# VectorE's program order in the last two units of a mixture-of-experts layer, and exact BF16 parts in the tables of its route

## The chip, the cores and the metric

One core of one Trainium2 chip runs the whole program. The metric is the device time of one execution in microseconds (us), as the median of several runs. The profile is one execution taken by the hardware profiler; "the profile" and "the trace" mean that execution. Engines are called TensorE (PE; its weight loads PEld), VectorE (DVE), ScalarE (ACT), GpSimd (POOL) and SyncE (SP, which issues most DMAs).

## The reference

Two layers work on 256 latent tokens and 256 context tokens of width 1024. Layer 0 mixes tokens by a bidirectional RG-LRU and gated linear attention, layer 1 by grouped-query attention. After the mixer, each layer has a hierarchical mixture of experts (MoE). What the change touches is the MoE of layer 0, over all 512 tokens:

```
p_group = softmax(t @ wg + bg);  w_group, g = top_k(p_group, 1)
e_val, e_idx = top_k(expert logits of group g, 2)
w_exp = softmax(e_val) * w_group
out = sum over the two experts e of  w_exp[e] * ((silu(t @ w1[e]) * (t @ w3[e])) @ w2[e])
x = x + gate * out
```

There are 16 experts (4 groups of 4), width 1024, hidden width 512, FP32 weights: 100.7 MB per layer.

## The kernel before

**Units.** Layer 0's route sorts the 16 experts by their number of tokens. The eight fullest get a unit of 128 slots each; the other eight share four units, two experts with 64 slots each. The 12 units run in the order of `SEQ` (line 23), unit 11 being a shared one. A unit gathers its tokens' rows from DRAM (`fetch_x`, 1660, an indirect DMA on GpSimd's queue), transposes them (`prep_x`, 1693), multiplies by w1 and w3 (`hidden`, 1737), forms silu times product (`he`), transposes that, and multiplies by w2 (`py`). For the full experts every FP32 operand is split into a high and a low part and each product is made of three (`mm3`); the low part of the transposed hidden row is `hl`, made on VectorE. Weights come as loads of 1 MB into slots that one list serves in order (`pump`, 201); a load is issued when TensorE, or the split of it, has read the slot's old content.

**How results come back.** Units 0 to 9 scatter their weighted rows to DRAM (`yd`). The last two units keep theirs in SBUF as `yh` and `yl`, and products with a transposed one-hot matrix (`finish_moe`, 1902) bring them to the tokens. What the other units scattered is fetched per token tile (`get_parts`, 1803: eight loads of 512 KB on GpSimd's queue, once unit 9's scatter has landed) and added on VectorE (`merge`, 1813).

**The route.** `unit_cols` (566) multiplies by `w_out` one token tile at a time; between the products `tick()` runs one closure of a queue (transposes of `xres`, router logits). `add_res` (1615) adds the residual, forms the row's scale (`scale`, a power on GpSimd and three VectorE steps) and writes the normalised, modulated row `h2` (`tile_`, 935) to DRAM. For the last tile, number 3 (`LATE_T`), half of that is put off to `route_end` (980). There ranks are counted with triangular BF16 products, and `to_units` (1077) makes the tables: one-hot matrices of slots (`oh`), values (`vals`), and FP32 products of both, which give each slot its token row (`ix`) and, in `weights_of` (1120), its weight (`wgt`). `experts` sorts the experts for SP's dynamic loads; `others` makes the weights and `cnt`.

**The branch.** If some expert has more tokens than slots (`cnt` over 0), spare passes run (1776 and 1777). They don't run here, but all engines load `cnt` and branch.

**What sets the order.** A scheduler orders each engine's instructions by estimated costs, and may move them past their place in the program. Between `pin(name)` calls the engines whose letter stands in `PIN` (61; p TensorE, d VectorE, a ScalarE, g GpSimd) keep program order among the instructions issued there. Units run under `m0`, with TensorE alone kept.

Of the kernel before, what the change touches and what calls it, by code (L numbers as in the profile page):

```python
# [10 lines left out]
F32 = mybir.dt.float32  # L11
# [49 lines left out]
PIN = dict(pair='p', px='padg', re='da', tb='dag', m0='p', n1='pad', xa='pad')  # L61
# [77 lines left out]
def backbone(ctx, tc, I, out):  # L139
# [426 lines left out]
    def unit_cols(name, b, hT, done, tokens_still, tiles=range(4), halves=(0, 1), after=None, on_act=True,  # L566
# [5 lines left out]
        if by_tile:  # L572
# [177 lines left out]
    rows2 = rt.tile([P, 2, 8], F32, name="rows2")  # L750

    def load_router():
# [87 lines left out]

    def route(l, NT, tmp, stream, h2_of, router):
# [49 lines left out]
        def logits(t, hf, part=None):  # L891
# [32 lines left out]
        def both(t):  # L924
            if l == 0 and t == NT - 2 and not queue:
# [9 lines left out]
        def tile_(t, late=False):  # L935
# [19 lines left out]
            todo = []  # L955
            for n in range(2):
                a = tmp("xa2")
                dve.scalar_tensor_tensor(a, x[:, n * 512:(n + 1) * 512], rss[t], A2[i][n], op0=ALU.mult, op1=ALU.mult)

                def shift(n=n, a=a):  # L960
                    dve.tensor_tensor(hv[:, n * 64:(n + 1) * 64, :], a.rearrange("q (p k) -> q p k", k=KD),
                                      B2[i][n].rearrange("q (p k) -> q p k", k=KD), op=ALU.add)
                if late and n:
                    todo.append(shift)
                else:
                    shift()

            def rest():
                for f in todo:
                    f()  # L970
                sp.dma_start(h2d[l][t * P:(t + 1) * P, :], h2)
            if late:
                return rest
            rest()
# [5 lines left out]
    def route_end(R, l, NT, early=None):  # L980
# [15 lines left out]

        def weights():
# [13 lines left out]
            wq = [st(f"wq{k}", 1) for k in range(2)]  # L1011
# [42 lines left out]
        pos, wq = None, None  # L1054

        def others():
# [4 lines left out]
            dve.tensor_copy(pos, R.pp)  # L1061
            cnt = rt.tile([P, 1], F32, tag="cnt", name="cnt")
# [11 lines left out]
        if l:  # L1074
            others()

        def to_units():
# [13 lines left out]
            oh = split_p.tile([P, 1024], F32R, tag="hi", name="oh").bitcast(F32).rearrange("p (n s) -> p n s", n=NK)  # L1091
# [11 lines left out]
            v = rt.tile([P, NK, 3, NU], F32, tag="vals", name="vals")  # L1103
            dve.tensor_tensor(v[:, :, 2, :], iota[:, 0:NU].unsqueeze(1).to_broadcast([P, NK, NU]),
                              uk.unsqueeze(2).to_broadcast([P, NK, NU]), op=ALU.is_equal)
# [27 lines left out]
            return ix, weights_of, (slots_, [v[:, k * NT:(k + 1) * NT] for k in range(2)])  # L1133
# [1377 lines left out]
```

## Time and profile before

| what | value |
|---|---|
| three runs | 1007.88, 1012.01, 1014.98 us; median 1012.01 |
| the profiled execution | 1008.28 us |
| its span | 1006.6 us |
| TensorE busy | 905.5 us (90%) |
| VectorE busy | 540.6 us (54%) |
| ScalarE busy | 396.5 us (39%) |
| moved by DMA | 304.56 MB, 303 GB/s over the span |
| granted TensorE clock, mean | 0.960 of 2.4 GHz |

The profiled execution's time is its span and 1.7 us around it. Busy shares are averages over stages with different limits: the route is a serial stretch of small instructions, the MoE parts read 100.7 MB of weights each. What a change in one stage is worth has to be read from that stage, from what its engines wait for last. Matmuls are pipelined, so a busy TensorE is not one at its peak.

### The profile page before, as it was taken

Reading aid. Unit: us, or ns where it says so; the run is one execution under the profiler, and the core shown is the slowest. Engines: PE = TensorE matmul, PEld = TensorE weight load, DVE = VectorE, ACT = ScalarE, POOL = GpSimd, SP = SyncE. Lnnn points to the kernel's source line nnn. Section 1 sums busy time; section 2 is a strip of 40 time slices with the busy share of each in tenths; the row PEclk is TensorE's granted clock in tenths of the full one; section 3 lists DMA queues with packets and bytes.
Section 4 is the critical chain, followed back from the end, with each engine's and each line's share of the span. In section 5 each row is a group of like instructions: output and inputs, shape, how many; then the busy total and the mean of one; then the engine's idle time right before and its main releaser. Section 6 shows DMA issues by size and latency. Waiting matters only on the chain. (4 is left out here: it accounts for less than half of the span.)

```text
span 1006.6 us, 12582 instructions
## 1 busy us (share of the span) xinstructions
PE 905.5 (90%) x4565; PEld 535.6 (53%) x4565; DVE 540.6 (54%) x1040; ACT 396.5 (39%) x686; POOL 130.3 (13%) x142
## 2 busy tenths in 40 slices
PE   5999989999964989999999377999996999999997
PEld 3556456667744647457568133764574444443442
DVE  5495777458684656428468357787656111111112
ACT  3465472234322637347468104543644221121210
POOL 1011520133302112100001100133001000000000
PEclk9999999999995999999999788999998899999999
DMA  9957353488453899999998957655758699999994
GB/s 311 385 177 271 126 209 124 170 299 299 147 185 137 309 418 419 419 420 411 415 420 347 402 211 291 257 208 211 271 200 334 231 416 418 415 417 414 417 413 159
DMA packets 63166, 304.56 MB, mean 303 GB/s; under 512 B 8579, under 2 KB 17667, under 8 KB 35057
## 3 DMA queue, kind: packets, MB, share of 16 engines
q1 hardware_dynamic: 55216, 284.56, 72.5%
q0 software_dynamic: 5120, 14.06, 3.6%
q10 hardware_dynamic: 2752, 4.98, 1.3%
q8 instruction: 40, 0.66, 0.3%
q14 instruction: 38, 0.30, 0.1%
HBM read 294.76 MB, written 12.58 MB: 305 GB/s over the span
## 5 line engine op out<-in xcount | busy, mean ns | idle before, releaser
L131 DVE TENSOR_TENSOR wlo<-raw,whi 128x1024 fp32r<-128x1024 f32 x144 | 174.3, 1231 | 64.7 <-ACT whi L131 62.4
L131 ACT ACTIVATE whi<-raw 128x1024 fp32r<-128x1024 f32 x140 | 145.6, 1057 | 99.5 <-PE acc L131 86.3
L131 PE MATMUL aux<-raw,x 128*64 128x512 f32 x488 | 116.3, 597 | 1.1 <-ACT x L131 0.7
L131 PEld LDWEIGHTS aux<-raw,x 128*64 128x64 f32 x488 | 34.4, 137 | 62.3 <-issue 58.4
L131 PE MATMUL acc<-raw,xf 128*64 128x512 f32 x256 | 61.9, 598 | 2.9 <-DMA raw<-in_w_dram 2.9
L131 PE MATMUL aux<-raw,sl 128*64 128x512 f32 x240 | 57.0, 594 | 0.7 <-ACT sl L131 0.7
L131 PE MATMUL ada<-raw,cT 128*32 128x512 f32 x320 | 56.4, 613 | 0.1
L131 PE MATMUL acc<-whi,xh 128*128 128x512 f32 x128 | 51.9, 405 | 0.0
L131 PE MATMUL acc<-wlo,xh 128*128 128x512 f32 x128 | 50.1, 391 | 0.8 <-DVE wlo L131 0.8
L131 PE MATMUL acc<-whi,xl 128*128 128x512 f32 x128 | 50.1, 391 | 0.0
L131 PE MATMUL acc<-whi,hl 128*128 128x512 f32 x64 | 26.4, 413 | 20.5 <-DVE hl L131 20.5
L131 DVE SCALAR_TENSOR_TENSOR aux<-aux,ws,mod 128x512 f32<-128x512 f32 x8 | 6.1, 758 | 71.6 <-PE aux L131 71.6
L131 PE MATMUL acc<-whi,h 128*128 128x512 f32 x128 | 43.1, 410 | 0.0
L131 PE MATMUL acc<-hhi,whi 128*128 128x512 f32 x96 | 37.0, 415 | 3.3 <-ACT hhi L131 2.8
L131 PEld LDWEIGHTS acc<-raw,xf 128*64 128x64 f32 x256 | 19.2, 136 | 38.6 <-issue 30.0
L131 DVE TENSOR_TENSOR he<-sl,aux 128x512 f32<-128x512 f32 x8 | 8.5, 1057 | 56.2 <-PE aux L131 56.2
L131 PE MATMUL acc<-raw,hf 128*64 128x512 f32 x128 | 34.5, 600 | 4.3 <-DMA raw<-in_w_dram 4.3
L131 POOL DMA_INDIRECT yd<-y,ix x10 | 11.9, 1192 | 198.5 <-ACT y L131 182.2
L131 PEld LDWEIGHTS aux<-raw,sl 128*64 128x64 f32 x240 | 17.8, 137 | 35.8 <-issue 33.7
L131 PE MATMUL acc<-hlo,whi 128*128 128x512 f32 x96 | 35.9, 409 | 0.0
L131 PE MATMUL acc<-hhi,wlo 128*128 128x512 f32 x96 | 35.0, 400 | 0.0
L131 ACT ACTIVATE x<-gat,B,A 128x256 f32<-128x256 f32 x26 | 13.3, 561 | 41.6 <-PE gat L131 40.8
(438 smaller groups left out, 1823.9 us busy)
## 6 DMA issues: line engine op xcount, KB each, us to landing
raw<-in_w_dram SPq DMA_DIRECT2D x151, 1024.0 KB, 15.0
raw<-in_w_ada_dram SPq DMA_DIRECT2D x38, 1024.0 KB, 5.4
raw<-in_w_dram SPq DMA_DIRECT2D x72, 512.0 KB, 12.1
raw<-in_w_in_dram SPq DMA_DIRECT2D x10, 1024.0 KB, 6.0
raw<-in_w_ada_dram SPq DMA_DIRECT2D x32, 256.0 KB, 7.6
raw<-in_w_qkv_dram SPq DMA_DIRECT2D x6, 1024.0 KB, 7.2
xres<-in_w_dram SPq DMA_DIRECT2D x5, 1024.0 KB, 8.4
raw<-in_w_out_dram SPq DMA_DIRECT2D x4, 1024.0 KB, 7.4
```

Source lines behind the costliest of these rows:

```text
L131: ins = f(*a, **k)
```

## The change

- Units 10 and 11 and the adds into `mod` that were held back run under a new pin `m1`, in which VectorE keeps program order too. All four merges stand behind the transposes of unit 11's hidden row; two of them stood ahead of its second w3 half.
- Tile 3's `h2` is made as (x times A2) on GpSimd in two halves, and (that times the row's scale, plus B2) on VectorE in two halves, the first after tile 3's logits, the second at the start of `route_end`.
- The `w_out` unit ticks after every weight part, and tile 2's remaining router steps always go through the queue.
- One-hot and value matrices become BF16; row numbers go as two exact parts (`rows4`: a multiple of 32 and the rest, loaded instead of computed), weights as three BF16 parts that sum to the FP32 value. Products are doubled and tripled accordingly.
- `cnt` is made ahead of `experts`; the weights' table is made behind the branch, at the head of the stretch `px`, in which TensorE, ScalarE, VectorE and GpSimd keep program order.

```diff
-PIN = dict(pair='p', px='padg', re='da', tb='dag', m0='p', n1='pad', xa='pad')
+PIN = dict(pair='p', px='padg', re='da', tb='dag', m0='p', m1='pd', n1='pad', xa='pad')
...
-                    if n % 2 or m == LATE_T and name == "w_out":
+                    if n % 2 or name == "w_out":
                         tick()
...
-        for n in range(2):
-            for k in range(2):
-                dve.tensor_scalar(rows2[:, n, 4 * k:4 * k + 4], tid, float(n * k * NTOK), None, op0=ALU.add)
+        sp.dma_start(rows4, I["rows4"])
...
+                if l == 0 and t == LATE_T:
+                    late_h2[1](0)
                 if part is None:
                     ends(t)
...
-            if l == 0 and t == NT - 2 and not queue:
+            if l == 0 and t == NT - 2:
...
+            if late:
+                def scaled(n):
+                    pool.tensor_tensor(hv[n], x[:, n * 512:(n + 1) * 512].rearrange("q (p k) -> q p k", k=KD), av[n],
+                                       op=ALU.mult)
+
+                def shifted(n):
+                    dve.scalar_tensor_tensor(hv[n], hv[n], rss[t], bv[n], op0=ALU.mult, op1=ALU.add)
+                    if n:
+                        sp.dma_start(h2d[l][t * P:(t + 1) * P, :], h2)
+                return scaled, shifted
...
-            oh = split_p.tile([P, 1024], F32R, tag="hi", name="oh").bitcast(F32).rearrange("p (n s) -> p n s", n=NK)
+            small = split_p.tile([P, 1024], F32R, tag="hi", name="oh").bitcast(BF16)
+            oh = small[:, 0:NK * P].rearrange("p (n s) -> p n s", n=NK)
...
-            for n in range(2):
-                dve.tensor_tensor(v[:, :, n, :], v[:, :, 2, :], rows2[:, n, :].unsqueeze(2).to_broadcast([P, NK, NU]),
-                                  op=ALU.mult)
+            dve.tensor_tensor(v, m.unsqueeze(2).to_broadcast([P, NK, 4, NU]),
+                              rows4.unsqueeze(3).to_broadcast([P, NK, 4, NU]), op=ALU.mult)
             one_hot(1)
             ps = aux()
             for n in range(NK):
-                pe.matmul(ps[:, 0:2 * NU], oh[:, n, :], v[:, n, 0:2, :].rearrange("p a u -> p (a u)"),
-                          start=(n == 0), stop=(n == NK - 1))
+                for c in range(2):
+                    pe.matmul(ps[:, 0:2 * NU], oh[:, n, :], v[:, n, 2 * c:2 * c + 2, :].rearrange("p a u -> p (a u)"),
+                              start=(n + c == 0), stop=(n + c == NK))
...
             def weights_of():
...
-                for k in range(2):
-                    m = v[:, k * NT:(k + 1) * NT, 2, :]
-                    dve.tensor_tensor(m, m, wq[k].to_broadcast([P, NT, NU]), op=ALU.mult)
+                dve.tensor_copy(part[:, :, 0], wqs)
+                dve.tensor_tensor(left, wqs, part[:, :, 0], op=ALU.subtract)
+                dve.tensor_copy(part[:, :, 1], left)
+                dve.tensor_tensor(part[:, :, 2], left, part[:, :, 1], op=ALU.subtract)
+                vw_ = vw[:, :, 0:3, :]
+                dve.tensor_tensor(vw_, m.unsqueeze(2).to_broadcast([P, NK, 3, NU]),
+                                  part.unsqueeze(3).to_broadcast([P, NK, 3, NU]), op=ALU.mult)
                 ps = aux()
                 for n in range(NK):
-                    pe.matmul(ps[:, 0:NU], oh[:, n, :], v[:, n, 2, :], start=(n == 0), stop=(n == NK - 1))
+                    for c in range(3):
+                        pe.matmul(ps[:, 0:NU], oh[:, n, :], vw[:, n, c, :], start=(n + c == 0), stop=(n + c == NK + 1))
...
             if n == 1:
+                if t == LATE_T:
+                    late_h2[0](1)
                 R.scale(t)
                 R.logits(t)
                 if t < LATE_T:
                     R.tile(t)
-                else:
-                    late_h2.append(R.tile(t, True))
+                if t == LATE_T - 1:
+                    late_h2.extend(R.tile(LATE_T, True))
+                    late_h2[0](0)
...
-    R.finish(lambda R: [f() for f in late_h2])
+    R.finish(lambda R: late_h2[1](1))
...
     for e in range(2):
         fetch_x(e)
+    R.count()
     R.experts()
...
     R.others()
-    wgt = weights_of()
...
     pin("px")
+    wgt = weights_of()
     prep_x(0)
...
     hidden(0, 0, 1)
+    pin("m1")
     for f in state["hold"]:
         f()
+    pin("m0")
...
         if e == NU - N_LAST:
+            pin("m1")
             get_parts()
         sl = wk.tile([P, 512], F32, tag="sl", name="sl")
         act.activation(sl, hs[e, 0], AF.Silu)
         hidden(e, 1, 0)
-        if e == NU - 1:
-            for t in F_ORDER[:2]:
-                merge(t)
         hidden(e, 1, 1)
...
         if e == NU - 1:
-            for t in F_ORDER[2:]:
+            for t in F_ORDER:
                 merge(t)
```

## Rows read from the trace of the kernel before

**Rows 1.** TensorE's waits by releaser: us in total, times, longest us.
```profile
PE acc L131 <- DVE hl L131: 20.5, 1, 20.5
...
PE aux L131 <- DVEq L1777: 4.2, 1, 4.2
```

**Rows 2.** Timeline of VectorE, 292 to 318 us: start, us, operation, [idle before].
```profile
292.22 0.69 DVE L131 TENSOR_TENSOR mod<-ada,mod 128x512 f32<-128x512 f32 x1 [0.44 <-PE ada L131]
...
293.69 0.74 DVE L131 SCALAR_TENSOR_TENSOR xa<-xres,r,row 128x512 f32<-128x512 f32 x1
...
296.36 0.28 DVE L131 TENSOR_TENSOR lT<-acc,lT 128x128 f32<-128x128 f32 x1
...
299.93 0.17 DVE L131 TENSOR_TENSOR cf<-aux,cfb 128x16 f32<-128x16 f32 x1
...
308.72 0.18 DVE L131 TENSOR_SCALAR ixf<-aux 128x24 f32<-128x24 f32 x1 [2.75 <-PE aux L131]
...
317.62 0.17 DVE L131 COPY wgt<-aux 128x12 f32<-128x12 f32 x1 [3.56 <-PE aux L131]
```

**Rows 3.** Stretches: us; busy of PE, PEld, DVE, ACT, POOL; PEclk, DMA share, GB/s.
```profile
300.00:305.00 5.00, 0.00 (x0) 0.00 (x0) 4.58 (x23) 0.00 (x0) 0.00 (x0) 0.50 0.26 105
...
585.00:590.00 5.00, 5.00 (x17) 3.95 (x16) 5.00 (x7) 0.00 (x0) 0.00 (x0) 0.70 0.01 6
```

**Rows 4.** Timeline of VectorE, 573 to 611 us.
```profile
573.43 1.23 DVE L131 TENSOR_TENSOR ya<-ya,yb 128x1024 f32<-128x1024 f32 x1 [15.40 <-issue]
...
580.80 1.23 DVE L131 TENSOR_TENSOR ya<-ya,yb 128x1024 f32<-128x1024 f32 x1 [3.56 <-DMA yb<-yd]
...
582.67 0.68 DVE L131 TENSOR_TENSOR hl<-aux,hh 128x512 fp32r<-128x512 f32 x1
...
609.19 0.75 DVE L131 SCALAR_TENSOR_TENSOR yl<-acc,wgt,yl 128x512 fp32r<-128x512 f32 x1 [10.19 <-ACT yl L131]
610.86 0.69 DVE L131 TENSOR_TENSOR pt<-acc,row 128x512 f32<-128x512 f32 x1 [0.92 <-PE acc L131]
```

**Rows 5.** Timeline of TensorE, 298 to 309 and 583 to 598 us.
```profile
298.82 0.28 PE L131 MATMUL aux<-Mb,tri 128*128 128x16 bf16 x5 [1.51 <-DVE Mb L131]
305.08 3.61 PE L131 MATMUL aux<-vals,oh 128*128 128x24 f32 x16 [5.98 <-DVE vals L131]
...
583.41 0.80 PE L131 MATMUL acc<-whi,hl 128*128 128x512 f32 x1 [20.50 <-DVE hl L131]
...
590.82 7.09 PE L131 MATMUL acc<-raw,xf 128*64 128x512 f32 x32
```

**Rows 6.** Timeline of SP's DMA issues, 590 to 595 us.
```profile
594.50 0.33 SPq L131 DMA_DIRECT2D raw<-in_w_dram  x1
```

**Rows 7.** Waits of SP's DMA queue by releaser: us in total, times, longest us.
```profile
SPq L131 <- PE acc L131: 108.4, 35, 31.1
```

**Rows 8.** DMA queues, 564 to 576 us: packets, MB, share of 16 engines (q0 GpSimd's).
```profile
q1 hardware_dynamic: 475, 3.47, 68.9%
q0 software_dynamic: 409, 1.54, 31.7%
```

**Rows 9.** Timeline of GpSimd, 69 to 76 us.
```profile
69.84 1.18 POOL L131 TENSOR_TENSOR q<-a 128x512 f32<-128x512 f32 x1 [4.15 <-ACT a L131]
```

**Rows 10.** Timeline of VectorE, 69 to 76 us.
```profile
70.03 1.53 DVE L131 SCALAR_TENSOR_TENSOR q<-q,th 128x512 f32<-128x512 f32 x1
...
73.76 0.68 DVE L131 SCALAR_TENSOR_TENSOR b<-b,u 128x512 f32<-128x512 f32 x1
```

**Rows 11.** The branch's line: operations, durations in ns (min/median/max), first and last start in us.
```profile
L1777 PEldq COMPARE_BRANCH  x1: 5688/5688/5688, 314.7 to 314.7; - x1
L1777 DVEq COMPARE_BRANCH  x1: 72/72/72, 318.3 to 318.3; - x1
...
L1777 DVEq EVENT_SEMAPHORE  x1: 21/21/21, 321.5 to 321.5; - x1
```

**Rows 12.** DMA queues, 317 to 320 us; q8 and q14 carry code.
```profile
q14 instruction: 4, 0.03, 3.4%
```

More of the change, by code (lines that the diff above doesn't have):

```diff
@@ L749, in backbone @@
     cfb = rt.tile([P, NE], F32, name="cfb")
-    rows2 = rt.tile([P, 2, 8], F32, name="rows2")
+    rows4 = rt.tile([P, 8, 4], F32, name="rows4")
     def load_router():
@@ L839, in router_of @@
         return rw, cb, c2
+    late_h2 = []
     def route(l, NT, tmp, stream, h2_of, router):
@@ L954, in tile_ @@
             hv = h2.rearrange("q (k p) -> q p k", k=KD)
-            todo = []
+            av, bv = ([r.rearrange("q (p k) -> q p k", k=KD) for r in m[i]] for m in (A2, B2))
+            hv = [hv[:, n * 64:(n + 1) * 64, :] for n in range(2)]
+            if late:
[7 more added lines that the diff above has]
+                return scaled, shifted
             for n in range(2):
@@ L958, in tile_ @@
                 dve.scalar_tensor_tensor(a, x[:, n * 512:(n + 1) * 512], rss[t], A2[i][n], op0=ALU.mult, op1=ALU.mult)
[L960 to L964, printed above, removed]
-                else:
[L966 to L974, printed above, removed]
+                dve.tensor_tensor(hv[n], a.rearrange("q (p k) -> q p k", k=KD), bv[n], op=ALU.add)
+            sp.dma_start(h2d[l][t * P:(t + 1) * P, :], h2)
         R.tile, R.logits, R.scale, R.halves_0 = tile_, both, scale, halves_0
@@ L995, in route_end @@
             pe.matmul(pp[:, 64:64 + NE], tri[:, 1, :], R.Mb[:, t, :], start=(t == 0), stop=(t == NT - 1))
+        pos, wq, wqs = None, None, None
         def weights():
@@ L1010, in weights @@
             dve.tensor_reduce(gs, ex, axis=AX.X, op=ALU.add)
-            wq = [st(f"wq{k}", 1) for k in range(2)]
+            nonlocal wqs
+            wqs = rt.tile([P, 2, NT, 1], F32, tag="wq", name="wq")
+            wq = [wqs[:, k] for k in range(2)]
+            wqs = wqs.rearrange("p k t o -> p (k t o)")
             m1, m2 = mk
@@ L1061, in others, with count @@
             dve.tensor_copy(pos, R.pp)
+        def count():
             cnt = rt.tile([P, 1], F32, tag="cnt", name="cnt")
@@ L1075, in route_end @@
             others()
+            count()
         def to_units():
@@ L1090, in to_units @@
             dve.tensor_reduce(pk, tm.rearrange("p k t e -> p (k t) e"), axis=AX.X, op=ALU.add)
-            oh = split_p.tile([P, 1024], F32R, tag="hi", name="oh").bitcast(F32).rearrange("p (n s) -> p n s", n=NK)
+            small = split_p.tile([P, 1024], F32R, tag="hi", name="oh").bitcast(BF16)
+            oh = small[:, 0:NK * P].rearrange("p (n s) -> p n s", n=NK)
+            v, vw = (small[:, a:a + NK * 12 * NU // 3].rearrange("p (n c u) -> p n c u", n=NK, u=NU)
+                     for a in (NK * P, NK * P + NK * 4 * NU))
             def one_hot(k):
@@ L1102, in to_units @@
             dve.tensor_reduce(uk, tm, axis=AX.X, op=ALU.add)
-            v = rt.tile([P, NK, 3, NU], F32, tag="vals", name="vals")
-            dve.tensor_tensor(v[:, :, 2, :], iota[:, 0:NU].unsqueeze(1).to_broadcast([P, NK, NU]),
+            m = rt.tile([P, NK, NU], F32, tag="vals", name="vals")
+            dve.tensor_tensor(m, iota[:, 0:NU].unsqueeze(1).to_broadcast([P, NK, NU]),
                               uk.unsqueeze(2).to_broadcast([P, NK, NU]), op=ALU.is_equal)
-            for n in range(2):
-                dve.tensor_tensor(v[:, :, n, :], v[:, :, 2, :], rows2[:, n, :].unsqueeze(2).to_broadcast([P, NK, NU]),
-                                  op=ALU.mult)
+            dve.tensor_tensor(v, m.unsqueeze(2).to_broadcast([P, NK, 4, NU]),
+                              rows4.unsqueeze(3).to_broadcast([P, NK, 4, NU]), op=ALU.mult)
             one_hot(1)
@@ L1122, in weights_of @@
                 w = rt.tile([P, NU], F32, name="wgt")
-                for k in range(2):
-                    m = v[:, k * NT:(k + 1) * NT, 2, :]
-                    dve.tensor_tensor(m, m, wq[k].to_broadcast([P, NT, NU]), op=ALU.mult)
+                left = rt.tile([P, NK], F32, tag="UK", name="left")
+                part = rt.tile([P, NK, 3], BF16, name="part")
+                dve.tensor_copy(part[:, :, 0], wqs)
[5 more added lines that the diff above has]
+                                  part.unsqueeze(3).to_broadcast([P, NK, 3, NU]), op=ALU.mult)
                 ps = aux()
                 for n in range(NK):
-                    pe.matmul(ps[:, 0:NU], oh[:, n, :], v[:, n, 2, :], start=(n == 0), stop=(n == NK - 1))
+                    for c in range(3):
+                        pe.matmul(ps[:, 0:NU], oh[:, n, :], vw[:, n, c, :], start=(n + c == 0), stop=(n + c == NK + 1))
                 dve.tensor_copy(w, ps[:, 0:NU])
@@ L1132, in to_units @@
             slots_ = [pk[:, k * NT:(k + 1) * NT].unsqueeze(2) for k in range(2)]
-            return ix, weights_of, (slots_, [v[:, k * NT:(k + 1) * NT] for k in range(2)])
+            return ix, weights_of, (slots_, [m[:, k * NT:(k + 1) * NT] for k in range(2)])
         def prepare(room=None):
@@ L1175, in tables @@
             return ix, w
-        R.M, R.prepare, R.tables, R.to_units, R.experts, R.others = M, prepare, tables, to_units, experts, others
+        R.M, R.prepare, R.tables, R.to_units, R.experts, R.others, R.count = (
+            M, prepare, tables, to_units, experts, others, count)
         return R
@@ L1611, in backbone @@
     R.AB = AB
-    late_h2 = []
     for n in range(2):
@@ L2492, in _layout @@
     f["tid"] = (np.arange(P)[:, None] + P * np.arange(4)[None] + 1).astype(np.float32)
+    rows = np.stack([np.concatenate([f["tid"], f["tid"]], 1), np.concatenate([f["tid"], f["tid"] + NTOK], 1)], -1)
+    f["rows4"] = np.concatenate([rows // 32 * 32, rows % 32], -1).astype(np.float32)
     for n in ("w1", "w3", "w2"):
```

4 lines of the change are left out of this document (1 added, 3 removed).

## The prediction

> **What bounds the kernel now.** I read three kinds of view. First the list of waits, for where TensorE stands still: one wait of 20.5 us for VectorE's `hl` and one of 4.2 us behind the branch [rows 1]. Both lie in layer 0's MoE part, and the diff touches both. Then the timelines around them. Last the DMA queues, to see what would be late next.
>
> **The first stretch**, 288 to 325 us, is one serial route: `xres` of the last token tile, router logits, ranks, tables of slots, gather, branch, first transposes. VectorE carries it [rows 2]; TensorE's short products wait in between at the lower of its two clock levels, 1.2 GHz (granted 0.50, [rows 3]).
>
> **The hole**, 562.9 to 583.4 us, is an order on VectorE, not a shortage. Before `hl` of unit 10 its queue has a merge that cannot start before 573.43 and one that waits for a DMA until 580.80; `hl` comes at 582.67 [rows 4]. TensorE's next product starts at 583.41 [rows 5]. Meanwhile the weights' loads stop too: the last one of the MoE is issued only at 594.50 [rows 6], after SP's longest wait for a slot that TensorE must read first, 31.1 us [rows 7]; between 585 and 590 us the DMA engines move next to nothing [rows 3].
>
> **The change, part by part.**
>
> *Kept order in units 10 and 11.* `hl` now precedes all merges. TensorE goes on at 562.9 instead of 583.4: 20.5 us come free. Not all of it stays; what is late next decides. Unit 10's w2 has 22 products left, some 5 us at 0.22 each (7.09 us for 32, [rows 5]), to 568. Unit 11's w3 takes 7.1 us, to 575; gate product and transposes some 2.5; then the first half of w2, 3.6, to some 581. The last weights go out when half of w3 is read, about 571.5. SP's queue moves 1.05 MB per 3.6 us there [rows 8] and, by my estimate, still holds three loads, so they are in near 586, and TensorE ends w2 near 589.
>
> But the merges now stand in program order *before* VectorE's `yl` of unit 11, and a merge needs its parts. The parts are eight loads of 0.52 MB on GpSimd's queue, 4.19 MB. While both queues have work, GpSimd's moves 1.54 MB in 12 us against 3.47 MB of SP's [rows 8], 0.128 MB/us. Before, SP's queue ran out first, and the parts were in by 586. Now four more loads of SP's (last weights, one `ada`, two `w_qkv`, 4.2 MB) start from 571.5 to 575, and its queue does not run out before the parts are in. At 576 some 2.65 MB of parts are left: 2.65 / 0.128 = 21 us, so the last part lands near 597. Its merge is two adds of 1.23 [rows 4] and two products of 0.69 like that at 610.86, 3.8 us: 600.8. Then two `yl`, 0.75 each [rows 4]: 602.3. The first product of the finish, at 610.86 before, comes right behind. **Worth 9 us.** Ends: with parts in at 586 as before, TensorE's weights decide (589) and 19 us remain; with half the share, parts land at 617 and 11 us are lost. I take 9, because the share is measured in this very stretch.
>
> *Held add.* The 0.69 us add into `mod` at 292.22 [rows 2] goes behind the branch, among splits that leave gaps.
>
> *Tile 3's shift on GpSimd, tile 2's router work earlier.* VectorE loses two scalings of 0.7 (there are two like that at 293.69, [rows 2]); both shifts stay, one right behind `lT`, one where it was. With the add that is 2.1 us less work ahead of `cf` (299.93), and `lT` of tile 3 waits behind less of it than until 296.36. Tile 2's turn, logits and ranking move under tile 3's products; nothing is added, the cover is tile 3's 24 products, and if it fails, `xres` of tile 3 is later by some 2 us of ranking. On GpSimd's queue the second half stands ahead of tile 3's power step: about 1.2 us later, under the transposes and logits.
>
> Against it stands a lock. Beside a GpSimd product that ends at 71.0 [rows 9], a VectorE instruction of the size that takes 0.68 takes 1.53 [rows 10]. Two GpSimd products of some 1.2 us can hold VectorE by 0.85 each. I charge one, as the other falls into the wait for TensorE: `cf` is **1.3 us** earlier (ends 2.1, and minus 1.6 with both and a failed cover).
>
> The Trainium skill (SBUF — State Buffer, "Who interferes with whom") says that a VectorE instruction with two SBUF inputs and a GpSimd one that reads SBUF exclude each other for the whole instruction. By that both halves would be charged, and the sum would lose another 0.85.
>
> *Tables in BF16.* The first table is 16 records in 3.61 us (eight FP32 products), and VectorE waits 2.75 us for it after its own last step [rows 2, 5]. BF16 products go some 0.03 apart at the higher clock (five in 0.28, [rows 5]); at the lower I take 0.055, so the eight that follow the last one-hot need 0.45 and some 0.35 to drain. One wide product in place of two small ones is no difference. **Minus 2 us** (ends 0 and 2.75). `rows4` is one more small load in SP's queue among the router's, tens of us before its use. `count`, four small steps, some 0.75 us, now precedes the experts' order and so SP's first load by it; that load's data is used units later.
>
> *Weights' table behind the branch.* Before, 16 records and a copy that ends at 317.8 [rows 2] made VectorE branch at 318.3, and its first instruction behind came at 321.5; TensorE stood 5.69 us in its own branch from 314.7 [rows 11]. The code packets come from 317 on, when the gathers' and weights' data have passed [rows 12]. So I let the branch end with the gathers, 3.3 us earlier by the two terms above, and VectorE no later than the rest (TensorE is through at 320.4), 0.8 us more. Behind it TensorE and VectorE keep program order: five VectorE steps of 0.17 to 0.5, some 1.3 us, then 24 BF16 products, 1.3 us, before the first transpose. Plus 2.6 (ends 1.3, and 6.7 at the 0.225 of the FP32 records in [rows 5]).
>
> Front: 1.3 + 2 + 0.8 - 2.6 = **1.5 us** earlier (ends 4.3 and minus 6). The units then follow at the same pace, since early loads are issued as unit 0 frees slots.
>
> **Sum.** 1.5 + 9 = 10.5 us. The profiled execution took 1008.28 us (span 1006.6): 997.8, so **998**. The three runs have their median 3.7 above it, at 1012.01 (1007.88 to 1014.98). After layer 0 I see nothing that takes it back: SP's loads there too are issued when a slot comes free, so they shift along.
>
> **Rivals.**
>
> *Forecast* (50%): 995 to 1002.
>
> *Fetch not queued* (10%). If a branch's code came at its own pace, VectorE would be through 3.2 us after its own branch, as before [rows 11], near 314, and the table would be made while the gathers fly: the 2.6 vanish, 995. For it: VectorE's short branch. Against it: TensorE's long one.
> The Trainium skill (Runtime: NRT & Kernel Launch, "Instruction fetch mechanics") says that a taken branch out of the fetched pages waits for a DMA fetch; it names no wait behind other DMAs.
>
> *Parts in time* (12%). If SP's extra loads do not slow the parts, the finish starts at 591 to 595: 16 to 20 us of hole, 987 to 991. For it: [rows 8] is one stretch only. Against: nothing shows why the share should rise.
>
> *Given back in front* (19%). The FP32-like price for the table behind the branch, the full lock, or parts 3 us later: 4 to 8 us remain, 1000 to 1004.
>
> *Not done* (3%): merges still before `hl`; then only the front, 1007. Against: `hl` is emitted within the kept stretch.
>
> *Slower* (6%). One mechanism: the merges in front of `yl`. It decides when the last part lands after 605 (610.86 less a merge and two `yl`): a share under 0.09 MB/us. At 0.05 the part lands at 629, 24 us past that: 1008.3 + 24 - 1.5 = 1031. For it: more `ada` and `w_qkv` loads follow as w2's slots come free. Against: with SP's queue full, [rows 8] already shows 0.128.
>
> **Range and chances.** 987 to 1007 leaves out the slower case and some of the others' ends, under 2 in 10. A measurement of this kernel tells 1%, some 10 us, from no change. The forecast straddles that; I put 40 of its 50 beyond, as the hole's end of 19 is far and the others near. With 9 of the fetch case and 12 of parts in time: faster 0.61. Same: 10 + 1 + 19 + 3 = 0.33. Slower: 0.06.
>
> **What would show it.** Right: no wait of TensorE for `hl`; merges after unit 11's `he`, with the last part about 10 us later after the scatter than before; `yl` of unit 11 directly behind the last merge; the first table under 1.5 us; transposes 2 to 3 us after VectorE's first step behind the branch. Wrong: a wait of over 3 us between unit 0's transposes and its products, parts past 605, or a new wait in the attention part as long as the one gained.

## The result, and the profile after

The changed kernel takes **998.62 us** (median of 4 runs, 997.22 to 999.94) against 1009.94 for the kernel before beside it (4 runs, 1007.85 to 1014.98): ratio 0.9875, 95% interval 0.9835 to 0.9915. Timed again in a later series it took 1001.88 (6 runs) against 1011.31 (11 runs): 0.9893, 0.9871 to 0.9914. The forecast was 998, between 987 and 1007. Against no change the result is clear; against the prediction's own mark of 1% for "faster" it is not, as the first interval holds 0.99. The profiled execution took 997.22 us, its span is 995.5.

TensorE's waits by releaser (us in total, times, longest us) answer to [rows 1]. The 20.5 us for `hl` are gone; 9.6 us for `yl` are new. The 12.3 for `oh` is the way through the branch up to the weights' table.

```profile
PE aux L131 <- DVE oh L131: 18.8, 3, 12.3
PE acc L131 <- DVE yl L131: 9.9, 2, 9.6
```

VectorE's timeline in unit 11 (start, us, operation, [idle before]) answers to [rows 4]: unit 11's `he`, the first add of each of the four merges, then `yl`, and the first product of the finish. The third and fourth merge wait for their parts; `yl` comes directly behind the last one.

```profile
574.51 1.03 DVE L131 TENSOR_TENSOR he<-sl,acc 128x512 f32<-128x512 f32 x1 [5.58 <-PE acc L131]
575.39 1.21 DVE L131 TENSOR_TENSOR ya<-ya,yb 128x1024 f32<-128x1024 f32 x1
...
581.05 1.23 DVE L131 TENSOR_TENSOR ya<-ya,yb 128x1024 f32<-128x1024 f32 x1 [1.87 <-DMA yb<-yd]
...
588.48 1.23 DVE L131 TENSOR_TENSOR pt<-pt 128x1024 f32<-128x1024 f32 x1 [3.61 <-DMA pt<-yd]
...
595.82 1.23 DVE L131 TENSOR_TENSOR pt<-pt 128x1024 f32<-128x1024 f32 x1 [3.53 <-DMA pt<-yd]
...
599.55 1.40 DVE L131 SCALAR_TENSOR_TENSOR yl<-acc,wgt,yl 128x512 fp32r<-128x512 f32 x2
601.18 0.69 DVE L131 TENSOR_TENSOR pt<-acc,row 128x512 f32<-128x512 f32 x1 [0.23 <-PE acc L131]
```

Stretches of the changed kernel (us; busy of PE, PEld, DVE, ACT, POOL; PEclk, DMA share, GB/s), the second for [rows 3]: from 585 to 590 us the DMA engines, at 0.01 before, are full, and TensorE's idle time has moved to 590 to 600.

```profile
325.00:330.00 5.00, 4.53 (x12) 3.02 (x12) 3.77 (x4) 3.04 (x4) 4.46 (x5) 0.50 0.63 173
...
585.00:590.00 5.00, 5.00 (x19) 1.44 (x18) 1.49 (x2) 1.38 (x2) 0.00 (x0) 1.00 1.03 430
...
595.00:600.00 5.00, 0.00 (x0) 0.00 (x0) 4.11 (x5) 0.00 (x0) 0.00 (x0) 0.50 1.01 426
```

Its DMA queues from 576 to 588 us (packets, MB, share of 16 engines) answer to [rows 8], and SP's last load of the MoE to [rows 6].

```profile
q1 hardware_dynamic: 465, 3.41, 67.2%
q0 software_dynamic: 464, 1.70, 34.6%
```

```profile
571.03 0.33 SPq L131 DMA_DIRECT2D raw<-in_w_dram  x1
```

In the front, VectorE's timeline (for [rows 2]): the first residual row of `w_out`'s second half, a small step that takes over 1.2 us, the last residual row, another such step, `rs_t` once more with nothing beside it, `cf`, the first table's readout `ixf` (which waits for nothing now), and the first step behind the branch.

```profile
259.96 1.28 DVE L131 TENSOR_TENSOR xres<-xres,y 128x512 f32<-128x512 f32 x2
...
288.33 1.25 DVE L131 SCALAR_TENSOR_TENSOR rs_t<-rs_t,ssq 128x1 f32<-128x1 f32 x1
...
294.27 0.69 DVE L131 TENSOR_TENSOR xres<-xres,y 128x512 f32<-128x512 f32 x1
...
295.30 1.22 DVE L131 COPY_PREDICATED ge<-upm,gt 128x80 f32<-128x80 int32 x1
...
297.72 0.16 DVE L131 SCALAR_TENSOR_TENSOR rs_t<-rs_t,ssq 128x1 f32<-128x1 f32 x1
...
302.75 0.16 DVE L131 TENSOR_TENSOR cf<-aux,cfb 128x16 f32<-128x16 f32 x1
...
309.05 0.18 DVE L131 TENSOR_SCALAR ixf<-aux 128x24 f32<-128x24 f32 x1
...
320.09 0.17 DVE L131 TENSOR_TENSOR left<-wq,part 128x8 f32<-128x8 f32 x1 [5.40 <-DVEq L1798]
```

GpSimd's two products beside those two small steps:

```profile
288.27 1.29 POOL L131 TENSOR_TENSOR h2x<-xres,row 128x512 f32<-128x512 f32 x1 [0.21 <-DMA h2d<-h2x]
295.04 1.38 POOL L131 TENSOR_TENSOR h2x<-xres,row 128x512 f32<-128x512 f32 x1 [5.48 <-DVE xres L131]
```

TensorE's tables and first transposes (for [rows 5]): 3.61 us became two times 0.4, of which one is behind the last one-hot.

```profile
308.02 0.37 PE L131 MATMUL aux<-oh 128*128 128x24 bf16 x8 [6.22 <-DVE oh L131]
308.62 0.39 PE L131 MATMUL aux<-oh 128*128 128x24 bf16 x8 [0.24 <-DVE oh L131]
321.32 0.79 PE L131 MATMUL aux<-oh 128*128 128x12 bf16 x24 [12.31 <-DVE oh L131]
321.96 3.65 PE L131 MATMUL aux<-ident,xg 128*128 128x128 f32 x16
```

The branch's line, now 1798 (for [rows 11]; operation, durations in ns, first and last start):

```profile
L1798 PEldq COMPARE_BRANCH  x1: 3508/3508/3508, 311.0 to 311.0; - x1
...
L1798 DVEq COMPARE_BRANCH  x1: 72/72/72, 314.5 to 314.5; - x1
...
L1798 DVEq EVENT_SEMAPHORE  x1: 21/21/21, 320.0 to 320.0; - x1
```

**The span, cut at four marks.** First residual row of the second half: 258.06 before, 259.96 after. From there to unit 0's `he`: 79.83 and 79.59. To unit 9's `he`: 198.76 and 196.31. To the first product of the finish: 74.21 and 65.32. To the end: 395.72 and 394.33. The differences are +1.90, -0.24, -2.45, -8.89 and -1.39; their sum is the 11.07 between the spans. The experiments show which of the five belong to the change. The marks are used below: "hole" is the fourth stretch.

### The profile page after: what moved, and what is told of

It is laid out like the page before. It is cut to its first block, busy times and chain, and to the rows that moved or that the text cites. A ratio compares the mean times of both kernels' runs of the same rounds, so it can differ in the third digit from the quotient of the medians.

```text
span 995.5 us, 12599 instructions
## 1 busy us (share of the span) xinstructions
PE 903.2 (91%) x4573; PEld 531.7 (53%) x4573; DVE 544.3 (55%) x1036; ACT 396.5 (40%) x686; POOL 133.5 (13%) x144
## 5 line engine op out<-in xcount | busy, mean ns | idle before, releaser
L131 PEld LDWEIGHTS aux<-raw,x 128*64 128x64 f32 x488 | 34.5, 136 | 62.1 <-issue 58.4
L131 PE MATMUL acc<-raw,hf 128*64 128x512 f32 x128 | 34.3, 600 | 4.0 <-DMA raw<-in_w_dram 4.0
L131 PEld LDWEIGHTS acc<-whi,xh 128*128 128x128 f32 x128 | 24.6, 192 | 8.5 <-issue 2.7
## 6 DMA issues: line engine op xcount, KB each, us to landing
raw<-in_w_dram SPq DMA_DIRECT2D x72, 512.0 KB, 11.1
```

The source lines that it names most:

```text
L131: ins = f(*a, **k)
```

## Experiments

Traces of single stretches are compared below by the same marks. Each kernel has one trace, the changed one has two, and kernels that share a stretch differ in it from trace to trace; where the difference is not far beyond that, both are given.

**One part at a time.** Only the kept order and the merges, on the kernel before. The held add goes with them, as its pin is `m1` too:

```diff
-PIN = dict(pair='p', px='padg', re='da', tb='dag', m0='p', n1='pad', xa='pad')
+PIN = dict(pair='p', px='padg', re='da', tb='dag', m0='p', m1='pd', n1='pad', xa='pad')
...
+    pin("m1")
     for f in state["hold"]:
         f()
+    pin("m0")
...
+            pin("m1")
             get_parts()
...
-            for t in F_ORDER[:2]:
-                merge(t)
...
-            for t in F_ORDER[2:]:
+            for t in F_ORDER:
```

> The kernel before with one part of the change alone: VectorE's kept order in units 10 and 11, all four merges behind unit 11's transposes; route, tables and branch as before. Theory (the hole carries the gain): no wait of TensorE for hl, the eight parts land some 3.7 us apart with the last near 597, yl of unit 11 at 600 to 602 and the first finish product near 602 against 610.86; 9 us less than before. Rival (the route carries a good part of the 12.5 us between the kernels): 5 us or less of gain, first product of the finish at 606 or later.

Measured: 1000.28 us (4 runs), ratio 0.9890 (0.9854 to 0.9927), so 7.4 to 14.8 us less than before. The hole is 65.99 us instead of 74.21, with the first finish product at 604.33 (602 was forecast; the start and the units took some 2.5 us more in this trace than with the change). The theory holds: the kept order alone gives the better part of the change.

```profile
604.33 0.69 DVE L131 TENSOR_TENSOR pt<-acc,row 128x512 f32<-128x512 f32 x1 [0.23 <-PE acc L131]
```

The trace shows one thing more. Up to the first table, all engines do the same in the same order as before, but for the add into `mod`, which VectorE no longer does there; and `cf` comes 40.75 us behind the first residual row, instead of 41.87. Out of the way, the add is worth 1.1 us.

Only the rest, on the changed kernel (the pin around the held add goes too):

```diff
-            pin("m1")
             get_parts()
...
         hidden(e, 1, 0)
+        if e == NU - 1:
+            for t in F_ORDER[:2]:
+                merge(t)
         hidden(e, 1, 1)
```

> The changed kernel with VectorE's kept order and the place of the merges undone: only route, tables and branch are new. Theory (the route gives next to nothing): TensorE waits some 20 us for hl again, the first finish product at 610 to 611, the time 0 to 1.5 us below before. Rival (the route gives what the prediction said or more): 1.5 to 4 us below before, the first finish product at 609 or earlier.

Measured: 1008.69 us (10 runs), ratio 0.9970 (0.9954 to 0.9987), so 1.3 to 4.7 us less than before, and the first finish product at 608.67: the numbers of the rival. Its reason is another matter. TensorE still waits for `hl`:

```profile
PE acc L131 <- DVE hl L131: 20.6, 1, 20.6
```

The hole is 73.82 us, 0.4 less than before. From the first residual row to unit 0's `he` it takes 79.22 us, 0.6 less than before. The rest of what its trace shows lies in the units, 196.24 us against 198.76, where all kernels do the same work. In the stretches from 350 to 500 us, DMA engines move 417 GB/s before and 421 after; but the kernel with SP's held loads (the fourth below), which up to 500 us issues the same as the changed one in the same order, has 418. The three rows are of the kernel before, the changed one and that one (columns as above):

```profile
350.00:500.00 150.00, 143.05 (x629) 86.40 (x628) 82.66 (x99) 78.04 (x98) 18.02 (x15) 1.00 1.01 417
```
```profile
350.00:500.00 150.00, 144.92 (x645) 89.30 (x644) 84.80 (x100) 80.10 (x100) 18.05 (x15) 1.00 1.01 421
```
```profile
350.00:500.00 150.00, 143.26 (x633) 86.44 (x632) 83.82 (x99) 78.94 (x98) 18.04 (x15) 1.00 1.01 418
```

The two traces with the old route have 198.8 and 199.1 us for the units; of eleven with the new one, ten have 196.2 to 197.2 and one, that kernel's, 198.6. So the pace can differ with the same instructions. Whether the route makes the better one likelier is **open**.

**Merges of tiles 2 and 3 behind the finish of tiles 0 and 1.**

```diff
-F_ORDER = (2, 3, 0, 1)
+F_ORDER = (0, 1, 2, 3)
-            for t in F_ORDER:
+            for t in F_ORDER[:2]:
...
-    pin("fin")
+    pin("m1")
     finish_moe(0)
     finish_moe(1)
+    merge(2)
+    merge(3)
+    pin("fin")
```

> The changed kernel with the parts fetched for tiles 0 and 1 first, and the merges of tiles 2 and 3 put behind yl of unit 11 and behind the finish of tiles 0 and 1, in VectorE's kept order. Theory (the last parts hold yl through the merges in front of it): part four lands near 581, so yl comes behind w2 near 588 and the first finish product near 590, 11 us earlier than with the change; the products of the next attention start when their weights are in, so 6 to 10 us less than the changed kernel. Rival (the loads of the attention's weights, landing until 604.6, set the start of that part): the finish is earlier but the time falls by less than 3 us.

Measured: 998.59 us (4 runs; 0.9864, 0.9829 to 0.9899), no clear gain on the changed kernel. The hole shrinks by 12.1 us to 53.20, and the stretch behind it grows by 13.2 to 407.50. TensorE's timeline shows where: the finish at 590.46, and then the second tile's transposes behind a wait of 8.84 us, as VectorE does both merges ahead of that tile's row.

```profile
590.46 1.19 PE L131 MATMUL acc<-yl,back 128*128 128x512 f32 x4
...
610.03 3.22 PE L131 MATMUL aux<-ident,pt 128*128 128x128 f32 x13 [8.84 <-DVE pt L131]
```

The first half of the theory holds (the parts held `yl`), the gain does not; the rival's time is right, but not its cause, since the wait is VectorE's, not a load's.

**SP's further loads behind the parts.** The next five of them (`N_HELD`) wait for the last part:

```diff
-                if state["behind"] is not None:
+                if state["behind"] is not None and state["held"] <= state["next"] < state["held"] + N_HELD:
                     pool.tensor_copy(r[:, 0:1], state["behind"])
                 load(r, src)
...
-        state["cap"] = len(order)
...
+        gate = rt.tile([P, 1], F32, name="gate")
+        pool.tensor_copy(gate, parts[F_ORDER[-1]][1][:, 0:1])
+        state["behind"], state["held"], state["cap"] = gate, state["cap"], len(order)
```

> The changed kernel with the loads that SP issues behind the last expert's weights (two of ada, three of w_qkv) made to wait, by a one-column copy on GpSimd, until the last part has landed. Theory (these loads take the parts' share of the DMA engines): the last part lands at 584 to 588 instead of 595.7, yl of unit 11 near 591, the first finish product near 592, 9 us earlier; the held loads are all in near 605 as before, as the DMA engines stay full, so 4 to 9 us less than the changed kernel. Rival (the parts have a pace of their own, 3.7 us each, whatever SP does): the last part lands near 595 again and the time is the same or, with the loads late, up to 10 us longer.

Measured: 999.08 us (4 runs; 0.9868, 0.9832 to 0.9905), the same as the changed kernel. The share is shown: the first four parts come 3.7 us apart as before; once SP's expert loads are all but in, at 584, the other four take 2.1, 2.1, 1.25 and 1.25 us, and VectorE hardly waits for the third merge. From 576 to 588 us GpSimd's queue moves 2.70 MB, instead of 1.70 with the change. But the held loads set the next start. TensorE has a product with `ada` in front of the finish, and for its weights it waits 6.71 us; meanwhile the DMA engines run dry. DMA queues, VectorE, DMA and TensorE of this kernel:

```profile
q0 software_dynamic: 744, 2.70, 56.1%
q1 hardware_dynamic: 296, 2.10, 42.2%
```

```profile
588.45 1.23 DVE L131 TENSOR_TENSOR pt<-pt 128x1024 f32<-128x1024 f32 x1 [0.41 <-DMA pt<-yd]
```
```profile
590.00:595.00 5.00, 1.96 (x8) 0.43 (x3) 4.90 (x7) 0.99 (x2) 3.63 (x6) 1.00 0.19 29
```
```profile
598.66 1.89 PE L131 MATMUL ada<-raw,cT 128*32 128x512 f32 x2 [6.71 <-DMA raw<-in_w_ada_dram]
```

So the theory's mechanism is right and its price wrong: it took the loads for free while they wait.

**The same two merges behind the norm**, as an edit of the kernel with two merges behind the finish:

```diff
     finish_moe(1)
-    merge(2)
-    merge(3)
-    pin("fin")
...
     norm1(1, (0, 1), ...)
...
+    for t in F_ORDER[2:]:
+        merge(t)
+    pin("fin")
```

> As the kernel with two merges behind, but the merges of tiles 2 and 3 stand behind the norm of tiles 0 and 1 as well, in VectorE's kept order. Theory (there the two merges only moved the wait: they held the second tile's row scale until 607.4, and TensorE waited 8.8 us for its transposes): the second tile's normalised row at 603 to 605 instead of 609.2, TensorE's wait for it under 4 us, and 4 to 8 us less than the changed kernel. Rival (the weights of the attention, landing until 607, or the merges and the norm of tiles 2 and 3 decide): the transposes are earlier, and the time is within 2 us of the changed kernel's.

Measured: 999.17 us (4 runs; 0.9883, 0.9847 to 0.9918). TensorE's wait for the second tile falls to 2 us and the attention's first products start at 604.4. Then the wait turns up one step on: tiles 2 and 3's rows are merged from 615.3 to 624.2 and their transposes come at 629.27, against 628.62 with the change (95.4 and 92.8 us behind unit 9's `he`). The rival holds, by its second cause.

```profile
602.09 2.61 PE L131 MATMUL aux<-ident,pt 128*128 128x128 f32 x11 [1.96 <-DVE pt L131]
...
629.27 0.87 PE L131 MATMUL aux<-ident,xn 128*128 128x128 f32 x3 [2.81 <-DVE xn L131]
```

**Three edits of the route, one trace each.**

```diff
-                    if n % 2 or name == "w_out":
+                    if n % 2 or m == LATE_T and name == "w_out":
-            if l == 0 and t == NT - 2:
+            if l == 0 and t == NT - 2 and not queue:
```

> The changed kernel with the ticks of the w_out unit as before: one after every second weight part but for the last tile, and tile 2's remaining router steps through the queue only if it is not empty. Theory (the ticks put the router's products and VectorE's ranking ahead of the last tiles' residual rows): from the first residual row of the second half to the last one 31.3 us as before instead of 34.3, and 10 to 11 us from there to cf instead of 8.5, so cf and the first table within 1 us of the changed kernel's, counted from the first residual row. Rival (GpSimd's halves make the stage longer): 34 us again.

Measured: 32.3 us from the first to the last residual row instead of 34.3, and still 8.4 from there to `cf`; `ixf` 47.0 us behind the first residual row instead of 49.1. The expectation is wrong: the ticks cost 2 us and give none back behind. The seven traces with the changed ticks and GpSimd's halves have 33.8 to 34.4 us for the first of these stretches and 48.6 to 49.3 for the last, so the cost is some 1.5 to 2 us. VectorE:

```profile
259.44 1.28 DVE L131 TENSOR_TENSOR xres<-xres,y 128x512 f32<-128x512 f32 x2
...
291.76 0.69 DVE L131 TENSOR_TENSOR xres<-xres,y 128x512 f32<-128x512 f32 x1
...
300.17 0.17 DVE L131 TENSOR_TENSOR cf<-aux,cfb 128x16 f32<-128x16 f32 x1
```

```diff
-                    pool.tensor_tensor(hv[n], x[...], av[n], op=ALU.mult)
+                    dve.tensor_tensor(hv[n], x[...], av[n], op=ALU.mult)
```

> The changed kernel with tile 3's two products by A2 on VectorE instead of GpSimd. Theory (beside GpSimd's products two VectorE instructions are stretched to 1.2 us, by some 0.5 to 1 each, and VectorE would need 0.7 for each product itself): no gain by GpSimd worth having, from the first residual row to cf within 0.7 us of the changed kernel's 42.8. Rival (the move to GpSimd saves its 1.4 us of VectorE): cf 1 to 1.5 us later. Rival (the lock costs more than the move saves): cf 0.7 to 1.5 us earlier.

Measured: `cf` 41.8 us behind the first residual row instead of 42.8. The last rival is the nearest: the two products on GpSimd cost VectorE more than the 1.4 us of work that they take from it, by 1.0 us against this one trace and by 0.4 to 1.0 against the six with the change in this stretch (42.3 to 42.8). So the sign is shown, the size only roughly. The rows above show how: `rs_t` of one element and `ge` of 80, 0.16 and 0.25 us elsewhere, end with GpSimd's product beside them (289.58 and 289.56; 296.52 and 296.42). The Trainium skill (SBUF — State Buffer, "Who interferes with whom") says that a VectorE instruction with two SBUF inputs contends with a GpSimd instruction that reads SBUF, and that this is an exclusive lock; the trace agrees, and by it both products are to be charged, not one.

```profile
261.29 1.28 DVE L131 TENSOR_TENSOR xres<-xres,y 128x512 f32<-128x512 f32 x2
...
303.12 0.17 DVE L131 TENSOR_TENSOR cf<-aux,cfb 128x16 f32<-128x16 f32 x1
```

```diff
     R.others()
+    wgt = weights_of()
...
     pin("px")
-    wgt = weights_of()
     prep_x(0)
```

> The changed kernel with the weights' table back ahead of the branch, still in BF16 parts. Theory (an engine gets its code behind the branch only when the gathers' rows have passed, near 320, whenever it branched): VectorE and TensorE are through at the same time as with the changed kernel, and the transposes of unit 0 come 1 to 2 us earlier, 11 to 12 us behind the first table's readout (ixf) instead of 12.9. Rival (each engine's way through the branch takes its own 3.5 to 5.5 us from where it starts): VectorE branches some 2 us later and all comes later by as much; the transposes 13 to 15 us behind ixf.

Measured: unit 0's transposes 12.05 us behind `ixf` (310.03) instead of 12.9, within the theory's range. VectorE does as the theory says: it is through the branch at 321.1, 11.1 us behind `ixf`, instead of 10.9 with the change, though it branched 2.3 us later. TensorE does not: behind the table it branches at 317.2 instead of 311.0, and is through 4.4 us later, at 321.7 instead of 314.5; that is 11.6 us behind `ixf` instead of 5.5. The trace puts the wait of its transposes down to the gathers' semaphore, but unit 0's rows, the first gather, land 4.5 us behind their issue at 311.6, that is at 316.1; what touches that semaphore last is a step of GpSimd on the branch's line, at 321.6. So what ends last is the branch, on TensorE and GpSimd, and not the rows. In the next kernel, with the table in the same place, the trace names the branch itself (last line).

```profile
316.40 0.78 PE L131 MATMUL aux<-oh 128*128 128x12 bf16 x24 [6.40 <-DVE oh L131]
322.08 3.32 PE L131 MATMUL aux<-ident,xg 128*128 128x128 f32 x16 [4.90 <-DMA xg<-h2d,ix]
```
```profile
L1799 PEldq COMPARE_BRANCH  x1: 4422/4422/4422, 317.2 to 317.2; - x1
...
L1799 DVEq EVENT_SEMAPHORE  x1: 21/21/21, 321.1 to 321.1; - x1
L1799 POOLq INC_SWDGE_SEM  x1: 436/436/436, 321.6 to 321.6; - x1
```
```profile
xg<-h2d,ix POOLq DMA_INDIRECT x1, 4.5
```
```profile
322.75 3.65 PE L131 MATMUL aux<-ident,xg 128*128 128x128 f32 x16 [5.03 <-PEq L1799]
```

**Together, beside the changed kernel again.** The three edits at once, by the three diffs above:

> The changed kernel with three edits of the route undone at once: ticks as before, tile 3's products by A2 on VectorE, the weights' table ahead of the branch; VectorE's kept order and the BF16 tables stay. Theory (the single looks add up: 2.0 us, 0.9 us and 0.9 to 2.4 us from the first residual row of the second half to unit 0's he, 79.6 us with the change): 75 to 76 us there, and 3 to 5 us less than the changed kernel beside it, some 995. Rival (the units behind run at the pace of the DMA engines and take it back): under 1.5 us less.

Measured: 997.50 us (5 runs, 992.09 to 1001.41; 0.9837, 0.9811 to 0.9862), 4.4 less than the changed kernel beside it by the medians, and the two intervals do not overlap, if barely. The theory's size holds for the time. From the first residual row to unit 0's `he` it takes 76.8 us (theory: 75 to 76), 2.8 less than in the changed kernel's two traces (79.6); but three other traces with the same front have 77.6 to 78.7, so 0.8 to 2.8 of the 4.4 are gained there. The rest I did not locate.

> The changed kernel itself, once more, as the measure for the two beside it. Theory: 998 to 999 us, ratio 0.986 to 0.989 to before; the stretches from the first residual row to ixf 49.1 us, from unit 9's he to the first finish product 65.3 us as in the other look, to 0.3 us; but the start of the program (TensorE's first gate product at 57.8 to 60.5 us) and the DMA engines' pace in the units (418 or 424 GB/s from 350 to 500 us) differ from look to look by 1 to 2.5 us whatever the kernel. Rival (these two differences belong to the kernels): 59.4 us and 424 GB/s again.

Measured: 1001.88 us, 0.9893, just above the expected ratios and 3 us above the expected time. The stretches are about as expected: 48.7 to `ixf` (0.4 less), 65.49 for the hole. The first gate product came at 61.97, so the start of the program does differ from trace to trace (57.8 to 62.0 over all kernels); the DMA pace was 422 again (the 424 of the expectation is 421 to 422 in the traces), so that half of the rival stays open, as above.

Last, the three edits and the merges placed where VectorE stands idle: tile 2's steps (`merge_steps`, the four steps of `merge` one at a time) between those of the finish, where it waits for ScalarE's sums, tile 3's in `norm1` between the two tiles' norm. Beside the three edits:

```diff
-F_ORDER = (2, 3, 0, 1)
+F_ORDER = (0, 1, 2, 3)
...
-            for t in F_ORDER:
+            for t in F_ORDER[:2]:
...
-    pin("fin")
-    finish_moe(0)
-    finish_moe(1)
+    pin("m1")
+    m2 = merge_steps(2)
+    finish_moe(0, (m2,))
+    finish_moe(1, (m2,))
...
             dve.tensor_tensor(xres[:, t, sl], xres[:, t, sl], y, op=ALU.add)
+            for f in fill:
+                next(f, None)
             square(t, n, ...)
...
+            if t == 0:
+                merge(3)
```

> The kernel with the three edits of the route undone, and beside that the parts of tiles 0 and 1 fetched and merged first, the steps of tile 2's merge put into the gaps of the finish of tiles 0 and 1 where VectorE waits for ScalarE, and tile 3's merge between the two tiles' norm. Theory (with the merges behind the norm, what came last was the norm of tiles 2 and 3 at 628 us, behind 7.6 us of merges): the first transposes of tiles 2 and 3's rows at 618 to 624 us instead of 627 to 629, and 4 to 8 us less than the kernel with the three edits alone. Rival (the transposes come earlier, but the attention's next loads or TensorE's products decide): within 2 us of it.

Measured: **990.24 us** (5 runs, 987.24 to 990.96), 0.9781 (0.9760 to 0.9803) to before: 2.2% below before and 11.6 us below the changed kernel. It is 7.3 us below the three edits alone, within the theory's 4 to 8. The theory's mark says less than I thought: the transposes of tiles 2 and 3 come at 624.89, 90.8 us behind unit 9's `he` against 94.8 with the three edits alone (92.8 to 94.8 over six traces with the merges as changed), but with two merges behind the finish they came after 87.8 us, and that kernel was no faster. A later mark shows the gain: TensorE's first product with the attention's output (`ohi`) comes 188.9 us behind unit 9's `he`, against 195.7 to 198.4 in the ten other traces with the kept order. Beside the kernel with the three edits alone, some 6 us of it are gained from 690 to 723 us, where TensorE spends 6.0 us on products with `ada` among the attention heads instead of 11.6; why fewer are left there, I did not test.

```profile
624.89 0.49 PE L131 MATMUL aux<-ident,xn 128*128 128x128 f32 x3
```

## Why the prediction was right

The time of 998 hits the first median to 0.6 us, and in that there is luck: the sum was taken from one execution of the kernel before, at 1008.28, while its medians in four series lie from 1009.94 to 1011.84, and the changed kernel took 1001.88 in the later one. The size of the change is what can be judged.

**The hole, 9 us: right, by its own steps.** No wait for `hl`; SP's last load at 571.03 (571.5 forecast); TensorE through with w2 at 587.4 (589). The step that decided was the share of the DMA engines: 0.128 MB/us from [rows 8], 0.142 in the rows after (1.70 MB in 12 us). The 0.128 is a little low, as [rows 8] begin before the parts come at their full pace (from 568 to 576 us they came at 0.141 before, too); and with the last part at 595.7 some 2.8 MB were left at 576, not 2.65: two small errors that cancel. The last part landed at 595.7 (597), the merge ended at 599.6 (600.8), the first product came at 601.18 (602). The stretch is 8.9 us shorter in this trace, 8.7 in the second, and 8.2 with the kept order alone. The share is shown by the kernel with the held loads, whose parts speed up when SP has nothing left.

The rows after also show what the share goes by, which the prediction did not ask. In those 12 us SP's queue moved 465 packets and GpSimd's 464: one for one, SP's of 7.3 KB and GpSimd's of 3.7. With the kept order alone it is 230 and 231 packets from 576 to 582 us. So GpSimd's third of the bytes fits two queues that take turns by packets; larger packets for the parts should raise it, which no run tested.

**The front, 1.5 us: the sum about right, its terms not.** From the first residual row to the first transposes it is 63.7 us before, and 62.0 and 62.1 in two traces after. But with the old route in the kept-order kernel it is 62.5 already: there the held add is out of the way. So some 1.1 of the 1.7 us are the add (priced at 0.7), and the edits of the route give half a us in sum (0 to 1.0 over five traces with the changed front); that the front came out near 1.5 is luck, as its terms cancelled. (Its low end, minus 6, adds up to minus 7.5.) By unit 0's `he` only 0.2 of the 1.7 is left: unit 0 ran at granted 0.50 from 325 to 330 us, where TensorE had 0.98 before, though the old route in the kept-order kernel had 0.50 there too. Five traces with the changed front differ by 2 us at that mark (77.6 to 79.6), so it can't show the front's gain.

- *`cf` 1.3 us earlier: this step failed.* Counted from the first residual row it is 0.9 later (0.4 to 1.0 over six traces), and against the kept-order kernel, which has the add out of the way too, 1.5 to 2.1 later. Two things that the working had taken as ends came true together: the cover by tile 3's products failed (1.5 to 2 us, the ticks), and there was a second lock (the halves on GpSimd cost 0.4 to 1.0 net). Both edits undone, `cf` is 40.5 us behind that row, 2.3 earlier.
- *Tables, 2 us: under-sized.* From `cf` to `ixf` 8.79 became 6.30, the same in all kernels with BF16 tables: 2.5. One reading in the working was wrong: the five BF16 products in 0.28 us stood at granted 0.50, the lower level, not the higher. So doubling their spacing was too much: at 0.50 eight products took 0.39 us (0.45 forecast) and 24 took 0.79 (1.3).
- *Branch and weights' table, 1.8 us lost: over-sized.* From `ixf` to the transposes 13.0 became 12.9, and 13.4 in the second trace. I let the branch end with the gathers. VectorE is through it 10.9 to 11.8 us behind `ixf` in all eleven traces with BF16 tables, whether it branched 5.5 or 7.8 us behind it, so the rival with a fetch at its own 3.2 us is out. In the same traces the first gather lands 6.1 to 6.7 us behind `ixf` and the second 10.6 to 12.7; that the second sets VectorE's exit is not shown. For TensorE the step was wrong: it is through 3.3 to 3.8 us after an early branch, and 4.4 to 4.9 after a late one. With the table behind the branch VectorE's exit and the table come last, with the table ahead the branch on TensorE and GpSimd; so the new place costs only the difference between the two, 12.9 to 13.7 us (eight traces) against 12.1 to 12.5 (three), not 2.6.

**Behind the hole, nothing taken back: right.** From the first finish product to the end it is 395.7 us before, 394.3 and 397.3 in two traces of the changed kernel, 393.9 and 396.3 in the kernels with one part. A spread of 3.4 us hides anything smaller. At a mark some 200 us behind unit 9's `he`, TensorE's first product with `ohi`, the gain is still whole: 206.8 us before and 206.4 with the route alone, 196.2 and 197.7 with the change, 196.7 with the kept order alone.

**So of the 11.07 us between the two spans** 8.9 are the hole and 0.2 the front. The start (+1.9), the units (-2.45) and the tail (-1.4) differ as much between traces of kernels that are alike there. The sum came out at 10.5 against 11.3 and 9.4 by the medians of two series: the size rests on one term that was worked out well; the front's terms cancelled. Of the signs, one was narrowly missed: the transposes came 1.9 us after VectorE's first step behind the branch, not 2 to 3.

**The rivals.** The merges in front of `yl` were the right thing to fear: they hold TensorE for 9.6 us, and with two of them elsewhere the finish comes 12.1 us earlier. The point named for a loss, a last part after 605, was not reached.

## What to carry to other kernels

When an order frees an engine, ask what each thing behind it now waits for, and price it by the transfers that start earlier than they did: here about half of 20.5 us went to loads that took the parts' share (with the parts in time the forecast had 19 us staying, and 8.9 stayed). Moving the step that waits (12 us won and lost again, twice) only moves the wait; a gain came when the same 7.6 us of work were cut into the gaps that VectorE has anyway. And when a wait may end by more than one thing, ask when each was done: the trace above put down to a gather what the branch had ended.

## What I had not expected of the hardware

Beside a GpSimd product a VectorE step of one element per partition takes as long as that product has left, 1.25 us instead of 0.16: the price is not in proportion to the step. TensorE, which branched while the first gather was being issued (311.0), got through in 3.5 us; VectorE, which branched at 314.5, took 5.4, but 3.2 when it branched 2.3 us later. Two DMA queues with work moved packets one for one (465 and 464), whatever the size of these. Four parts of 0.52 MB that had come 3.7 us apart came 1.25 to 2.1 us apart once SP's queue was all but empty. And kernels with the same instructions up to there read the same weights at 418 or 421 to 422 GB/s in different executions (350 to 500 us), 2.3 us over the units.
